# Transposes moved from TensorE to VectorE in a batched x·yᵀ kernel: 32x32 blocks, cross-partition casts and block-diagonal 128x128 weights

## Chip, cores, metric

One core of one Trainium2 chip. The metric is the device time of a whole execution in microseconds (us), median of several runs. The spans in the profiles are about 2 us shorter than these times. In profiles PE is TensorE (matmuls), DVE is VectorE, ACT is ScalarE, POOL is GpSimd, and SP issues the transfers of the 16 DMA engines, which move data in packets. SBUF holds the tiles of these kernels, PSUM the results of their matmuls, and to evict is to copy a result from PSUM to SBUF.

## The reference

```python
x: (8, 12, 512, 64) float32      # batch, heads, t, channels
y: (8, 12, 512, 64) float32      # batch, heads, s, channels
out = np.einsum('bhtc,bhsc->bhts', x, y).astype(np.float32)   # (8, 12, 512, 512)
```

There are 96 independent products of 512x64 by 64x512. The inputs are 25 MB, the output is 101 MB. Both kernels give the matmul its operands with the 64 channels, over which it sums, on partitions, although memory has them along rows. How that transpose is done is what the change is about.

## The kernel before

Twelve groups of eight heads. POOL casts to bf16, TensorE transposes 128x128 blocks into PSUM, VectorE and ScalarE copy them out, TensorE multiplies in 64x64 tiles, VectorE and ScalarE evict, and the SP queue stores 2 MB at a time.

```python
xs = lpool.tile([P, 2, R, C], fp32)                  # R = 16 rows: load runs of 4 KB
nc.sync.dma_start(xs.rearrange("p a r c -> p a (r c)"), xv[g])
...
nc.gpsimd.tensor_copy(b[:, rows], s[:, :, rows].rearrange("p a r c -> p r a c"))   # cast
...
for k in range(K):
    nc.tensor.transpose(pt[:, k, :], yb[:, half * K + k].rearrange("p a c -> p (a c)"), ident)
dst = yT[:, :, half * K:(half + 1) * K]
src = pt.rearrange("p k n -> p n k")                 # scattered read of PSUM, runs of 16 bytes written
nc.vector.tensor_copy(dst, src)                      # or nc.scalar.activation, in turn
...
nc.tensor.matmul(pm[h * 64:(h + 1) * 64, two, :], xT[...], yT[...], start=True, stop=True)
...
if k % 2 == 0: nc.scalar.activation(ot[:, 2 * k:2 * k + 2, :], pm, COPY)
else:          nc.vector.tensor_copy(ot[:, 2 * k:2 * k + 2, :], pm)
nc.sync.dma_start(ov[g, 2 * a + pair], otf)          # 16 KB runs
```

Of the kernel before, what the change touches and what calls it, by code (L numbers as in the profile page):

```python
# [1 line left out]

# [5 lines left out]


@with_exitstack  # L10
def kernel(
    ctx: ExitStack,
    tc: tile.TileContext,
    x: bass.AP,
    y: bass.AP,
    out: bass.AP,
):





    nc = tc.nc
    B, H, T, C = x.shape
    _, _, S, _ = y.shape
    P = 128
    G = 4
    Q = P // G
    R = T // Q
    NG = B * H // (2 * G)  # L30
    K = R // 2
    AHEAD = 3
    fp32 = mybir.dt.float32
    bf16 = mybir.dt.bfloat16
    COPY = mybir.ActivationFunctionType.Copy
    assert C * 2 == P and S == T and R == 16

    xv = x.rearrange("b h t c -> (b h t c)").rearrange("(g a p n) -> g p a n", a=2, p=P, n=R * C)
    yv = y.rearrange("b h t c -> (b h t c)").rearrange("(g a p n) -> g p a n", a=2, p=P, n=R * C)
    ov = out.rearrange("b h t s -> (b h t s)").rearrange("(g a p n) -> g a p n", a=4, p=P, n=K * S)  # L40

    const = ctx.enter_context(tc.tile_pool(name="const", bufs=1))
    lpool = ctx.enter_context(tc.tile_pool(name="lpool", bufs=AHEAD))
    bpool = ctx.enter_context(tc.tile_pool(name="bpool", bufs=2))
    tpool = ctx.enter_context(tc.tile_pool(name="tpool", bufs=2))
    opool = ctx.enter_context(tc.tile_pool(name="opool", bufs=6))
    ptpool = ctx.enter_context(tc.tile_pool(name="ptpsum", bufs=2, space=bass.MemoryType.PSUM))
    pmpool = ctx.enter_context(tc.tile_pool(name="pmpsum", bufs=3, space=bass.MemoryType.PSUM))

    loaded = {}  # L50

    def load(g):
        xs = lpool.tile([P, 2, R, C], fp32)
        ys = lpool.tile([P, 2, R, C], fp32)
        nc.sync.dma_start(ys.rearrange("p a r c -> p a (r c)"), yv[g])  # L55
        nc.sync.dma_start(xs.rearrange("p a r c -> p a (r c)"), xv[g])  # L56
        loaded[g] = (xs, ys)

    for g in range(AHEAD):
        load(g)  # L60

    ident = const.tile([P, P], bf16)
    make_identity(nc, ident)

    def prepare(g, made):

        xs, ys = loaded.pop(g)
        yb = bpool.tile([P, R, 2, C], bf16)
        xb = bpool.tile([P, R, 2, C], bf16)
        for s, b in ((ys, yb), (xs, xb)):  # L70
            for half in range(2):
                rows = slice(half * K, (half + 1) * K)
                nc.gpsimd.tensor_copy(b[:, rows], s[:, :, rows].rearrange("p a r c -> p r a c"))  # L73
        if g + AHEAD < NG:
            load(g + AHEAD)
        yield
        yT = tpool.tile([P, G * Q, R], bf16)
        xT = tpool.tile([P, K, P, 2], bf16)
        for half in range(2):
            pt = ptpool.tile([P, K, P], bf16)  # L80
            for k in range(K):
                nc.tensor.transpose(  # L82
                    pt[:, k, :], yb[:, half * K + k].rearrange("p a c -> p (a c)"), ident
                )
            dst = yT[:, :, half * K:(half + 1) * K]
            src = pt.rearrange("p k n -> p n k")
            if half == 0:
                nc.vector.tensor_copy(dst, src)  # L88
            else:
                nc.scalar.activation(dst, src, COPY)  # L90
            yield
        for half in range(2):
            pt = ptpool.tile([P, K, P], bf16)
            for k in range(K):
                e, i = divmod(k, K // 2)
                nc.tensor.transpose(  # L96
                    pt[:, k, :], xb[:, e * K + half * K // 2 + i].rearrange("p a c -> p (a c)"), ident
                )
            dst = xT[:, half * K // 2:(half + 1) * K // 2]
            src = pt.rearrange("p (e i) n -> p i n e", e=2)  # L100
            if half == 0:
                nc.vector.tensor_copy(dst, src)  # L102
            else:
                nc.scalar.activation(dst, src, COPY)  # L104
            yield
        made[g] = (xT, yT.rearrange("p n k -> p (n k)"))

    made = {}
    for _ in prepare(0, made):
        pass  # L110
    for g in range(NG):
        xT, yT = made.pop(g)
        steps = prepare(g + 1, made) if g + 1 < NG else iter(())
        for a in range(2):
            for pair in range(2):
                ot = opool.tile([P, K, S], fp32)
                otf = ot.rearrange("p r s -> p (r s)")
                edge = (g == 0 and a == 0) or (g == NG - 1 and a == 1)
                for k in range(K // 2):
                    if (pair * K // 2 + k) in (0, 3, 6):  # L120
                        next(steps, None)
                    pm = pmpool.tile([P, 2, S], fp32)
                    for two in range(2):
                        for h in range(2):
                            col = (2 * pair + h) * Q
                            nc.tensor.matmul(  # L126
                                pm[h * 64:(h + 1) * 64, two, :],
                                xT[a * C:(a + 1) * C, 2 * k + two, col:col + Q].rearrange("c n e -> c (n e)"),
                                yT[a * C:(a + 1) * C, (2 * pair + h) * S:(2 * pair + h + 1) * S],
                                start=True, stop=True,  # L130
                            )
                    if k % 2 == 0:
                        nc.scalar.activation(ot[:, 2 * k:2 * k + 2, :], pm, COPY)  # L133
                    else:
                        nc.vector.tensor_copy(ot[:, 2 * k:2 * k + 2, :], pm)  # L135
                    if edge and k % 2 == 1:
                        i, j = (2 * k - 2) * S, (2 * k + 2) * S
                        nc.sync.dma_start(ov[g, 2 * a + pair][:, i:j], otf[:, i:j])
                if not edge:
                    nc.sync.dma_start(ov[g, 2 * a + pair], otf)  # L140


# [1 line left out]
_INS = ['x', 'y']  # L144
_OUTS = [((8, 12, 512, 512), 'float32')]


# [23 lines left out]
```

## Time and profile before

| | before |
|---|---|
| time, median | 306.78 us (3 runs); 306.69 us over the 4 runs beside the changed kernel |
| share of the span in which the DMA engines carry the kernel's data | 98.2% |
| VectorE, ScalarE, POOL busy | 145, 119, 49 us |

The kernel is bound by its DMA; the lines that carry this are in the prediction. Beside them the groups of VectorE: line, engine, operation, tiles, shapes, count, then busy us and mean ns of one.

```profile
L135 DVE COPY ot<-pm 128x1024 f32<-128x1024 f32 x96 | 117.2, 1223 | 113.3 <-PE pm L126 57.3
...
L102 DVE COPY xT<-pt 128x1024 bf16<-128x1024 bf16 x12 | 14.7, 1223 | 10.8 <-PE pt L96 9.4
L88 DVE COPY yT<-pt 128x1024 bf16<-128x1024 bf16 x12 | 14.6, 1216 | 8.9 <-PE pt L82 8.9
```

Three kinds of copy, contiguous and rearranged, cost the same 1.2 us for 1024 elements.

### The profile page before, as it was taken

The page shows a single profiled execution, that of the slowest core. Times are in us where ns is not written, and L with a number is a line of the kernel's source. Part 1 is how long each engine was busy: PE and PEld are TensorE (multiplying, and loading weights), DVE is VectorE, ACT ScalarE, POOL GpSimd, SP SyncE. Part 2 cuts the span into 40 slices and gives each one's busy share as a digit, 9 for nine tenths or more (in the row PEclk, how much of TensorE's full clock was granted, in tenths as well). Part 3 has the DMA queues.
Part 4 walks back from the last instruction along what each step waited for, and adds up shares of the span by engine and source line. Part 5 has one row for each costly group of instructions (what it writes and reads, how often), then busy time and mean ns, then how long its engine had stood idle before and what let it go on. Part 6 is the DMA issues. An engine that isn't in the chain of part 4 may idle for free.

```text
span 304.3 us, 2968 instructions
## 1 busy us (share of the span) xinstructions
PE 208.5 (69%) x1152; PEld 104.6 (34%) x1152; DVE 144.7 (48%) x120; ACT 119.4 (39%) x121; POOL 49.3 (16%) x54
## 2 busy tenths in 40 slices
PE   0899999999959538928946844893897797671000
PEld 0444344555425114513613522541453443330000
DVE  0456666567446435616525733743565664443000
ACT  1454645364445224624515512542364552522000
POOL 3773220400500310230050050031000000000000
PEclk9999999999999855555555655555555555555555
DMA  7999999999999999999999999999999999999992
GB/s 283 411 410 418 436 429 423 419 442 405 445 419 419 430 431 421 420 437 424 426 426 435 414 429 433 413 433 429 433 433 429 431 433 429 428 428 433 423 420 89
DMA packets 14031, 126.03 MB, mean 414 GB/s; under 512 B 1216, under 2 KB 1216, under 8 KB 7360
## 3 DMA queue, kind: packets, MB, share of 16 engines
q1 hardware_dynamic: 14016, 125.83, 98.2%
q8 instruction: 9, 0.15, 0.2%
q14 instruction: 6, 0.05, 0.0%
HBM read 25.17 MB, written 100.66 MB: 413 GB/s over the span
## 4 chain that ended last, share of the span: by engine, by line
DMA 60%; PE 23%; DVE 4%; ACT 2%; issue 1%; POOL 1%; SPq 0%; ACTq 0%
DMA out_dram<-ot 48%; PE pm L126 17%; DMA xs<-in_x_dram 12%; PE pt L82 3%; PE pt L96 3%; DVE ot L135 2%; ACT ot L133 2%; DVE xT L102 1%; POOL xb L73 1%; SPq L55 0%; ACTq L133 0%; SPq L140 0%; ACT xT L104 0%; SPq L56 0%
## 5 line engine op out<-in xcount | busy, mean ns | idle before, releaser
L126 PE MATMUL pm<-yT,xT 64*64 64x512 bf16 x768 | 164.0, 610 | 56.0 <-ACT ot L133 53.9
L135 DVE COPY ot<-pm 128x1024 f32<-128x1024 f32 x96 | 117.2, 1223 | 113.3 <-PE pm L126 57.3
L133 ACT ACTIVATE ot<-pm 128x1024 f32<-128x1024 f32 x96 | 95.1, 1023 | 113.7 <-DMA out_dram<-ot 81.2
L126 PEld LDWEIGHTS <-xT 64*64 64x64 bf16 x768 | 66.1, 150 | 131.2 <-issue 122.7
L73 POOL CAST yb<-ys 128x1024 bf16<-128x1024 f32 x24 | 24.3, 1040 | 140.5 <-DMA ys<-in_y_dram 94.7
L82 PE MATMUL pt<-ident,yb 128*128 128x128 bf16 x192 | 23.7, 307 | 10.7 <-POOL yb L73 6.9
L73 POOL CAST xb<-xs 128x1024 bf16<-128x1024 f32 x24 | 24.3, 1040 | 16.3 <-issue 6.9
L82 PEld LDWEIGHTS <-yb 128*128 128x128 bf16 x192 | 19.9, 143 | 20.3 <-issue 11.5
L96 PE MATMUL pt<-ident,xb 128*128 128x128 bf16 x192 | 24.9, 310 | 1.1 <-POOL xb L73 0.9
L96 PEld LDWEIGHTS <-xb 128*128 128x128 bf16 x192 | 19.1, 141 | 19.3 <-issue 17.8
L104 ACT ACTIVATE xT<-pt 128x1024 bf16<-128x1024 bf16 x12 | 12.3, 1024 | 32.9 <-PE pt L96 29.4
L102 DVE COPY xT<-pt 128x1024 bf16<-128x1024 bf16 x12 | 14.7, 1223 | 10.8 <-PE pt L96 9.4
L88 DVE COPY yT<-pt 128x1024 bf16<-128x1024 bf16 x12 | 14.6, 1216 | 8.9 <-PE pt L82 8.9
L90 ACT ACTIVATE yT<-pt 128x1024 bf16<-128x1024 bf16 x12 | 12.3, 1022 | 9.3 <-PE pt L82 7.7
L90 ACT ACT_TABLE_LOAD x1 | 1.3, 1283 | 0.7 <-PEq L155 0.7
masks.py:199 POOL TENSOR_SCALAR_AFFINE_SELECT ident<-ident 128x128 bf16<-128x128 bf16 x1 | 0.3, 292 | 0.1
masks.py:197 POOL MEMSET ident<- 128x128 bf16 x1 | 0.2, 204 | 0.3 <-POOLq L155 0.3
L155 POOL MEMSET const-float32-0.0<- 128x1 f32 x1 | 0.1, 98 | 0.2 <-issue 0.2
L155 POOL MEMSET const-bfloat16-1.0<- 128x1 bf16 x1 | 0.1, 101 | 0.0
L155 POOL MEMSET const-uint8-127<- 128x1 uint8 x1 | 0.1, 101 | 0.0
L155 POOL MEMSET const-float32-1.0<- 128x1 f32 x1 | 0.1, 98 | 0.0
## 6 DMA issues: line engine op xcount, KB each, us to landing
out_dram<-ot SPq DMA_DIRECT2D x44, 2048.0 KB, 28.3
ys<-in_y_dram SPq DMA_DIRECT2D x12, 1024.0 KB, 20.3
xs<-in_x_dram SPq DMA_DIRECT2D x12, 1024.0 KB, 22.2
out_dram<-ot SPq DMA_DIRECT2D x8, 1024.0 KB, 21.0
```

The lines of the kernel that those rows point to most:

```text
L73: nc.gpsimd.tensor_copy(b[:, rows], s[:, :, rows].rearrange("p a r c -> p r a c"))
L82: nc.tensor.transpose(pt[:, k, :], yb[:, half * K + k].rearrange("p a c -> p (a c)"), ident)
L88: nc.vector.tensor_copy(dst, src)
L90: nc.scalar.activation(dst, src, COPY)
L96: nc.tensor.transpose(pt[:, k, :], xb[:, e * K + half * K // 2 + i].rearrange("p a c -> p (a c)"), ident)
L102: nc.vector.tensor_copy(dst, src)
L104: nc.scalar.activation(dst, src, COPY)
L126: nc.tensor.matmul(pm[h * 64:(h + 1) * 64, two, :], xT[a * C:(a + 1) * C, 2 * k + two, col:col + Q].rearrange("c n e -> c (n e)"), yT[a * ...
L133: nc.scalar.activation(ot[:, 2 * k:2 * k + 2, :], pm, COPY)
L135: nc.vector.tensor_copy(ot[:, 2 * k:2 * k + 2, :], pm)
L155: nc = _bacc.Bacc("TRN2", target_bir_lowering=False, num_devices=1)
```

## The change

The intent is to take the transposes and their evictions off TensorE and PSUM. Two heads share one 128x128 matmul: each is split into two channel halves, the four pieces lie on four blocks of 32 partitions, and the weights hold zeros where the heads differ. VectorE's transpose does this in blocks of 32x32, from SBUF to SBUF. Its output is written so that both operands stand in exactly the order that the matmul wants.

```diff
-    G = 4 ... R = T // Q          # 16 rows per partition and head group
+    G = 8 ... R = T // Q          # 32 rows: load runs of 8 KB
-                nc.gpsimd.tensor_copy(b[:, rows], s[:, :, rows].rearrange("p a r c -> p r a c"))
+        for ch in range(2):
+            for u in range(2):     # 32 partitions at a time, to another block of partitions
+                cast(engines[n % len(engines)], xb[(2 * ch + u) * D:(2 * ch + u + 1) * D, :, :, u, :], ...)
...
-                nc.tensor.transpose(pt[:, k, :], yb[...], ident)      # and the same for x, and evictions
+        nc.vector.transpose(
+            xT.rearrange("p k h m -> p (k h m)").rearrange("p (k r i) -> p k i r", k=K, i=2 * E),
+            xb.rearrange("p k e u c -> p k (e u) c"),
+        )
+        nc.vector.transpose(yT.rearrange("p (r j) -> p j r", j=R), yb)
...
-                                pm[h * 64:(h + 1) * 64, two, :], ...   # 768 matmuls, 64x64
+                    pm[:, two, :], xT[:, k + two, h, :], yT[:, h * S:(h + 1) * S], ...   # 384, 128x128
-                    if k % 2 == 0:  # ScalarE and VectorE in turn
+            if k == 4:              # VectorE one of four, else ScalarE
-    opool bufs=6
+    opool bufs=7
...
+    with tc.manual_schedule():      # instruction order as written; edge stores no longer divided
```

More of the change, by code (lines that the diff above doesn't have):

```diff
@@ L6 @@
 from concourse._compat import with_exitstack
-from concourse.masks import make_identity
 @with_exitstack
@@ L26 @@
     P = 128
-    G = 4
+    G = 8
     Q = P // G
     R = T // Q
-    NG = B * H // (2 * G)
-    K = R // 2
+    NG = B * H // G
+    K = 8
+    E = R // K
+    D = 32
     AHEAD = 3
@@ L35 @@
     COPY = mybir.ActivationFunctionType.Copy
-    assert C * 2 == P and S == T and R == 16
-    xv = x.rearrange("b h t c -> (b h t c)").rearrange("(g a p n) -> g p a n", a=2, p=P, n=R * C)
-    yv = y.rearrange("b h t c -> (b h t c)").rearrange("(g a p n) -> g p a n", a=2, p=P, n=R * C)
-    ov = out.rearrange("b h t s -> (b h t s)").rearrange("(g a p n) -> g a p n", a=4, p=P, n=K * S)
+    assert C == 2 * D and S == T and R == D and Q * 2 == D
+    xv = x.rearrange("b h t c -> (b h t c)").rearrange("(g p n) -> g p n", p=P, n=R * C)
@@ L42 @@
+    yv = y.rearrange("b h t c -> (b h t c)").rearrange("(g p n) -> g p n", p=P, n=R * C)
+    ov = out.rearrange("b h t s -> (b h t s)").rearrange(
+        "(o u h q n) -> o h q u n", u=2, h=2, q=Q * E, n=K * S
+    )
     const = ctx.enter_context(tc.tile_pool(name="const", bufs=1))
     lpool = ctx.enter_context(tc.tile_pool(name="lpool", bufs=AHEAD))
-    bpool = ctx.enter_context(tc.tile_pool(name="bpool", bufs=2))
-    tpool = ctx.enter_context(tc.tile_pool(name="tpool", bufs=2))
-    opool = ctx.enter_context(tc.tile_pool(name="opool", bufs=6))
@@ L47 @@
-    ptpool = ctx.enter_context(tc.tile_pool(name="ptpsum", bufs=2, space=bass.MemoryType.PSUM))
-    pmpool = ctx.enter_context(tc.tile_pool(name="pmpsum", bufs=3, space=bass.MemoryType.PSUM))
-    loaded = {}
+    ybpool = ctx.enter_context(tc.tile_pool(name="ybpool", bufs=2))
+    tpool = ctx.enter_context(tc.tile_pool(name="tpool", bufs=4))
+    opool = ctx.enter_context(tc.tile_pool(name="opool", bufs=7))
+    pmpool = ctx.enter_context(tc.tile_pool(name="pmpsum", bufs=4, space=bass.MemoryType.PSUM))
@@ L52, in load @@
+    loaded, made = {}, {}
+    zeroed = [const.tile([P, K, E, 2, D], bf16, name=f"xb{half}") for half in range(2)]
     def load(g):
-        xs = lpool.tile([P, 2, R, C], fp32)
-        ys = lpool.tile([P, 2, R, C], fp32)
-        nc.sync.dma_start(ys.rearrange("p a r c -> p a (r c)"), yv[g])
-        nc.sync.dma_start(xs.rearrange("p a r c -> p a (r c)"), xv[g])
+        xs = lpool.tile([P, R, C], fp32)
+        ys = lpool.tile([P, R, C], fp32)
+        nc.sync.dma_start(xs.rearrange("p r c -> p (r c)"), xv[g])
+        nc.sync.dma_start(ys.rearrange("p r c -> p (r c)"), yv[g])
@@ L57, in load @@
         loaded[g] = (xs, ys)
-    for g in range(AHEAD):
-        load(g)
-    ident = const.tile([P, P], bf16)
-    make_identity(nc, ident)
-    def prepare(g, made):
-        xs, ys = loaded.pop(g)
-        yb = bpool.tile([P, R, 2, C], bf16)
-        xb = bpool.tile([P, R, 2, C], bf16)
-        for s, b in ((ys, yb), (xs, xb)):
-            for half in range(2):
-                rows = slice(half * K, (half + 1) * K)
-                nc.gpsimd.tensor_copy(b[:, rows], s[:, :, rows].rearrange("p a r c -> p r a c"))
-        if g + AHEAD < NG:
-            load(g + AHEAD)
-        yield
-        yT = tpool.tile([P, G * Q, R], bf16)
-        xT = tpool.tile([P, K, P, 2], bf16)
-        for half in range(2):
-            pt = ptpool.tile([P, K, P], bf16)
-            for k in range(K):
-                nc.tensor.transpose(
-                    pt[:, k, :], yb[:, half * K + k].rearrange("p a c -> p (a c)"), ident
-                )
-            dst = yT[:, :, half * K:(half + 1) * K]
-            src = pt.rearrange("p k n -> p n k")
-            if half == 0:
-                nc.vector.tensor_copy(dst, src)
-            else:
-                nc.scalar.activation(dst, src, COPY)
-            yield
-        for half in range(2):
-            pt = ptpool.tile([P, K, P], bf16)
-            for k in range(K):
-                e, i = divmod(k, K // 2)
-                nc.tensor.transpose(
-                    pt[:, k, :], xb[:, e * K + half * K // 2 + i].rearrange("p a c -> p (a c)"), ident
-                )
-            dst = xT[:, half * K // 2:(half + 1) * K // 2]
-            src = pt.rearrange("p (e i) n -> p i n e", e=2)
-            if half == 0:
-                nc.vector.tensor_copy(dst, src)
-            else:
-                nc.scalar.activation(dst, src, COPY)
-            yield
-        made[g] = (xT, yT.rearrange("p n k -> p (n k)"))
@@ L108 @@
-    made = {}
-    for _ in prepare(0, made):
-        pass
-    for g in range(NG):
-        xT, yT = made.pop(g)
-        steps = prepare(g + 1, made) if g + 1 < NG else iter(())
-        for a in range(2):
-            for pair in range(2):
-                ot = opool.tile([P, K, S], fp32)
-                otf = ot.rearrange("p r s -> p (r s)")
-                edge = (g == 0 and a == 0) or (g == NG - 1 and a == 1)
-                for k in range(K // 2):
-                    if (pair * K // 2 + k) in (0, 3, 6):
-                        next(steps, None)
-                    pm = pmpool.tile([P, 2, S], fp32)
-                    for two in range(2):
-                        for h in range(2):
-                            col = (2 * pair + h) * Q
-                            nc.tensor.matmul(
-                                pm[h * 64:(h + 1) * 64, two, :],
-                                xT[a * C:(a + 1) * C, 2 * k + two, col:col + Q].rearrange("c n e -> c (n e)"),
-                                yT[a * C:(a + 1) * C, (2 * pair + h) * S:(2 * pair + h + 1) * S],
-                                start=True, stop=True,
-                            )
-                    if k % 2 == 0:
-                        nc.scalar.activation(ot[:, 2 * k:2 * k + 2, :], pm, COPY)
-                    else:
-                        nc.vector.tensor_copy(ot[:, 2 * k:2 * k + 2, :], pm)
-                    if edge and k % 2 == 1:
-                        i, j = (2 * k - 2) * S, (2 * k + 2) * S
-                        nc.sync.dma_start(ov[g, 2 * a + pair][:, i:j], otf[:, i:j])
-                if not edge:
-                    nc.sync.dma_start(ov[g, 2 * a + pair], otf)
@@ new lines, in cast, with casts @@
+    def cast(engine, dst, src):
+        if engine is nc.scalar:
+            nc.scalar.activation(dst, src, COPY)
+        else:
+            engine.tensor_copy(dst, src)
+    def casts(g, half, engines):
+        xs, ys = loaded[g]
+        xb = zeroed[half]
+        base = half * 64
+        n = 0
+        for ch in range(2):
+            for u in range(2):
+                lo = base + u * D
+                src = xs[lo:lo + D, :, ch * D:(ch + 1) * D]
+                cast(
+                    engines[n % len(engines)],
+                    xb[(2 * ch + u) * D:(2 * ch + u + 1) * D, :, :, u, :],
+                    src.rearrange("p (e k) c -> p k e c", k=K),
+                )
+                n += 1
+        yb = ybpool.tile([P, R, D], bf16)
+        for ch in range(2):
+            cast(
+                engines[n % len(engines)],
+                yb[ch * 64:(ch + 1) * 64],
+                ys[base:base + 64, :, ch * D:(ch + 1) * D],
+            )
+            n += 1
+        return xb, yb
@@ new lines, in transposes, with result @@
+    def transposes(g, half, xb, yb):
+        xT = tpool.tile([P, K, 2, P], bf16)
+        nc.vector.transpose(
+            xT.rearrange("p k h m -> p (k h m)").rearrange("p (k r i) -> p k i r", k=K, i=2 * E),
+            xb.rearrange("p k e u c -> p k (e u) c"),
+        )
+        yT = tpool.tile([P, 2 * S], bf16)
+        nc.vector.transpose(yT.rearrange("p (r j) -> p j r", j=R), yb)
+        made[g, half] = (xT, yT)
+    def result(g, half, h, steps):
+        xT, yT = made[g, half]
+        ot = opool.tile([P, K, S], fp32)
+        for k in range(0, K, 2):
+            next(steps, None)
+            pm = pmpool.tile([P, 2, S], fp32)
+            for two in range(2):
+                nc.tensor.matmul(
+                    pm[:, two, :], xT[:, k + two, h, :], yT[:, h * S:(h + 1) * S], start=True, stop=True
+                )
+            if k == 4:
+                nc.vector.tensor_copy(ot[:, k:k + 2, :], pm)
+            else:
+                nc.scalar.activation(ot[:, k:k + 2, :], pm, COPY)
+        nc.sync.dma_start(ov[2 * g + half, h], ot.rearrange("p r s -> p (r s)"))
@@ new lines, in prepare @@
+    def prepare(g):
+        b = {}
+        for step in range(16):
+            if step in (0, 1):
+                b[step] = casts(g, step, [nc.gpsimd])
+            if step in (5, 13):
+                transposes(g, step // 8, *b[step // 8])
+            if step == 12 and g + AHEAD < NG:
+                load(g + AHEAD)
+            yield
+    with tc.manual_schedule():
+        for g in range(AHEAD):
+            load(g)
+        nc.vector.memset(zeroed[0], 0.0)
+        nc.gpsimd.memset(zeroed[1], 0.0)
+        b0 = casts(0, 0, [nc.vector, nc.scalar, nc.gpsimd])
+        transposes(0, 0, *b0)
+        b1 = casts(0, 1, [nc.gpsimd, nc.scalar])
+        transposes(0, 1, *b1)
+        if AHEAD < NG:
+            load(AHEAD)
+        for g in range(NG):
+            steps = prepare(g + 1) if g + 1 < NG else iter(())
+            for half in range(2):
+                for h in range(2):
+                    result(g, half, h, steps)
+            for _ in steps:
+                pass
```

## The prediction

> **What bounds the kernel now.** I first read the 40 slices of the span, because the busy shares of the page (PE 69%, DVE 48%, ACT 39%, POOL 16%) name no engine as the limit:
>
> ```profile
> DMA  7999999999999999999999999999999999999992
> GB/s 283 411 410 418 436 429 423 419 442 405 445 419 419 430 431 421 420 437 424 426 426 435 414 429 433 413 433 429 433 433 429 431 433 429 428 428 433 423 420 89
> ...
> q1 hardware_dynamic: 14016, 125.83, 98.2%
> ...
> out_dram<-ot SPq DMA_DIRECT2D x44, 2048.0 KB, 28.3
> ```
>
> From the second slice to the last but one the 16 DMA engines are never idle, and they spend 98.2% of the span on the kernel's own 125.83 MB (25.17 read, 100.66 written). The last line says that a 2 MB store takes 28.3 us from issue to landing. At 430 GB/s 2.10 MB takes 4.88 us, so 28.3/4.88 = 5.8 stores stand in the queue: all six output buffers are full, and the engines run ahead of the DMA as far as buffers allow.
>
> Next the waits, to see whether any engine holds the queue up:
>
> ```profile
> ACT ot L133 <- DMA out_dram<-ot: 81.2, 22, 8.6
> DVE ot L135 <- DMA out_dram<-ot: 55.4, 20, 7.8
> PE pm L126 <- ACT ot L133: 53.9, 21, 8.2
> ```
>
> Both evicting engines wait for a store to free its buffer, 137 us together, and PE waits behind them. Everything queues behind the stores. Then the busy table by stretch, at both ends and in the middle:
>
> ```profile
> 5.00:20.00 15.00, 11.70 (x74) 6.37 (x75) 6.79 (x6) 5.12 (x5) 11.40 (x12) 1.00 1.02 412
> ...
> 200.00:270.00 70.00, 52.21 (x266) 25.82 (x263) 37.76 (x32) 30.05 (x31) 4.05 (x4) 0.50 1.01 430
> 295.00:297.00 2.00, 0.00 (x0) 0.00 (x0) 0.00 (x0) 0.00 (x0) 0.00 (x0) 0.50 0.92 389
> 297.00:300.00 3.00, 0.00 (x0) 0.00 (x0) 0.00 (x0) 0.00 (x0) 0.00 (x0) 0.50 0.34 145
> 300.00:303.00 3.00, 0.00 (x0) 0.00 (x0) 0.00 (x0) 0.00 (x0) 0.00 (x0) 0.50 0.12 49
> ```
>
> Columns: stretch, length, then PE, PEld, DVE, ACT, POOL busy, granted clock, DMA share, GB/s. Three things: the pure-load start runs at 412 GB/s, the store-rich middle at 430; halving the granted PE clock at 100 us changed nothing; and the end is a ramp of 6 us in which only some of the 16 DMA engines still work (49 GB/s is two of them).
>
> The trace's record of single packets says why. Median duration: 4,096 bytes 159 ns, 8,192 bytes 309 ns, 16,384 bytes 611 ns. So each packet costs about 9 ns (2 x 159 - 309) on top of its bytes. The sixteen landings of each DMA say the rest: at the first load the slowest DMA engine is 0.5 us behind the fastest, at the last store 6.6 us[...]. The lag grows in steps, of which the clearest follow packets that are not the kernel's data:
>
> ```profile
> q8 instruction: 9, 0.15, 0.2%
> q14 instruction: 6, 0.05, 0.0%
> ```
>
> Nine packets of 16,384 bytes are 147,456 bytes; PE has 1152 + 1152 instructions, which makes exactly 64 bytes each. So q8 is PE's program being fetched, 256 instructions at a time. Each fetch holds one DMA engine for about 0.94 us, and the lag of that engine jumps by 0.6 to 1.3 us. The slowest engine sets the end.
>
> [...]the trace before has none, but its DVE copies (1024 elements, 1223 ns) give the rate I use[...].
>
> **The change, part by part.** 12 groups of 8 heads as before, per group 2 loads of 1 MB and 4 stores of 2 MB. DMA pace of a group: 2 x 2.45 + 4 x 4.86 = 24.3 us (4.86 is the spacing of 2 MB landings, 2.45 that of the 1 MB stores made of 8 KB packets).
> - Compute per group, against 24.3. POOL: 12 casts of 1024 elements per partition, at 1040 ns each as before (the cost goes by elements per partition, so narrower casts are no cheaper): 12.5 us, up from 4.2. ACT: 12 evictions x 1.023 = 12.3. DVE: 4 evictions x 1.223 = 4.9, plus 2 x (2048-element transpose[...] 2.29, and 1024-element 1.22) = 7.0, sum 11.9. PE: 32 matmuls of 512 columns, at 0.43 each (spacing seen for two of the old ones, an upper value): 13.7. All transposes on PE, their PSUM and their evictions go. Every engine is at half the DMA's pace, so all of this lies beside the DMA: 0 us.
> - Load packets of 8 KB for 4 KB: 6,144 become 3,072. In landings, 1 MB of loads took 2.56 us in the pure-load start and about 2.49 among stores; 8 KB packets took 2.445. Ten loads x 0.11 + fourteen x 0.045 = 1.7 us saved. The edge stores become 16 KB: 8 x 0.015 = 0.1.
> - PE's program: 384 matmuls + 384 weight loads = 768 instructions, 3 fetches for 9. Six fetches of about 1 us fall away from the 16 engines; the slowest engine probably bore three or four of the nine and now one or two. I take 2 us off its lag of 6.6.
> - Start: the first result needs casts, DVE transposes and then ACT, which does casts of the second half first. Loads land at about 5.8 and 8.4 us; casts of the first half end near 9.5, ACT's last cast near 12.5, evictions run until about 16, first store near 16 us. The first eight loads keep the DMA busy until about 22.6 us (23.4 before), so it has 6 us to spare. Next stores by my schedule near 22, 26 and 32 us, due at 27.5, 32 and 37: tight, but fed.
> - End: with seven buffers the last stores are queued some 30 us ahead, so the undivided 2 MB edge stores cost nothing. 0 us.
>
> Sum: -1.8 - 2.0 = -3.8 us; 306.8 - 3.8 = 303.0.
>
> **Rivals.**
> 1. Nothing but the packets counts: lag comes from elsewhere too (part of it grows between fetches, at the loads among stores). For it: all jumps together are 33 us over 16 engines, nine fetches explain perhaps 10. Then about 305.
> 2. The lag shrinks more[...]: the slowest engine lags only 3 us. Then 301, at the edge of 2%.
> 3. POOL becomes the bound. Its casts triple, narrow, and shift between partitions; if a 32-partition cast took twice 1040 ns, POOL would need 25 us per group against 24.3, and the time would be about 315. Against it: the old cast with a permuted source already costs only about 1 ns per element.
> 4. [...]For it: the DRAM side has 64 rows of 2 heads instead of 128.[...] Against it:[...] rows stay 16 KB and the order by partition is kept.
> 5. The start starves the DMA: a delay of the first or second store beyond the 6 us in hand would cost 1 to 4 us.
>
> **Range and chances.** Rivals 1 and 2 set the inside of the range: 301 to 305, widened to 300 and 307 for rival 5 and the run-to-run spread. Faster by over 2% means below 300.8, for which the lag must nearly vanish: 0.17. Slower by over 2% needs rival 3 or 4: 0.12. Within 2%: 0.71.
>
> **What would show it.** Right: DMA slices all at 9 from the second on; 8 KB packets at 309 ns, 16 KB at 611; the instruction queue at 3 packets of 16 KB in place of 9; start stretch above 420 GB/s; ramp at the end of 4 to 5 us instead of 6; POOL near 150 us, ACT near 152, DVE near 143 busy; stores about 6.5 deep. Wrong: a DMA share below 0.9 in the middle (POOL or DVE bound, and SP waiting for evictions while the stores land in 5 to 10 us), 16 KB packets well above 611 ns[...], or a hole between 16 and 40 us (start).

The sum: 1.7 us for load packets and 0.1 for edge stores, 2.0 for PE's program, nothing for compute, together -3.8 us and 303.0. The 2.29 us of the longer transpose belongs to compute; it used a rate that no trace shows; contig_only measured 2.30 later. The trace before has no transpose of VectorE. In rival 2 its 3 us was a guess. Rival 4 is that the new store pattern slows the stores down. That a cast's time goes by its elements per partition was assumed; the page after shows it, 1039 ns on 32 partitions and 1034 on 64, for 1040 on 128 before. The nine fetch packets took 0.89 to 1.11 us each; only after some of them is the slowest DMA engine further behind.

## The result, and the profile after

| | before | after |
|---|---|---|
| time, median | 306.69 us (306.30 to 306.85, 4 runs) | 449.05 us (449.01 to 449.14, 4 runs) |
| ratio | | 1.4645, 95% interval 1.462 to 1.467 |

The outputs are right. All eight runs are fast (none is over 1.5% above the fastest of its kernel). Ratios here and below are the mean time of one kernel's fast runs over that of the other's of the same rounds, so not quite the ratio of the medians. The prediction, 303.0 us and 300 to 307, was far off.

The page of the changed kernel: busy line, two rows of slices, the data queue's share, store landings.

```profile
PE 140.9 (32%) x384; PEld 49.7 (11%) x384; DVE 384.8 (86%) x99; ACT 144.6 (32%) x150; POOL 144.1 (32%) x142
...
DVE  5999999999889898898898988988989889889630
...
DMA  8904399597688498298298487667844826628497
...
q1 hardware_dynamic: 10368, 125.83, 68.1%
...
out_dram<-ot SPq DMA_DIRECT2D x48, 2048.0 KB, 7.8
```

The DMA row, a wall of nines before, is full of holes; 68.1% replaces 98.2%. A store lands 7.8 us after its issue in place of 28.3, so the queue is nearly empty. VectorE is busy nearly everywhere. ScalarE and POOL, at 145 and 144 us, are near what I had worked out (152 and 150); VectorE is at 385 in place of 143. Its groups say where:

```profile
L98 DVE STREAM_TRANSPOSE xT<-xb 128x2048 bf16<-128x2048 bf16 x24 | 222.3, 9263 | 0.3 <-ACT xb L66 0.3
...
L103 DVE STREAM_TRANSPOSE yT<-yb 128x1024 bf16<-128x1024 bf16 x24 | 115.9, 4828 | 0.0
L118 DVE COPY ot<-pm 128x1024 f32<-128x1024 f32 x48 | 62.8, 1313 | 41.1 <-issue 36.2
```

The transposes take 9.26 and 4.83 us; I had 2.29 and 1.22. Together that is 338 us, more than the whole kernel before. The waits follow from it:

```profile
ACT ot L120 <- PE pm L114: 281.0, 52, 11.6
PE pm L114 <- DVE ot L118: 265.9, 25, 12.6
POOL xb L68 <- DVE xT L98: 225.7, 22, 11.3
```

ScalarE waits for matmuls, matmuls wait for VectorE's one eviction in four, and POOL waits for the transpose to free its buffer: each wait is up to 12 us long, about as long as a pair of transposes. VectorE's order in time (start us, us) shows one half group (four heads, two stores):

```profile
206.00 1.23 DVE L118 COPY ot<-pm 128x1024 f32<-128x1024 f32 x1 [2.01 <-issue]
207.14 9.26 DVE L98 STREAM_TRANSPOSE xT<-xb 128x2048 bf16<-128x2048 bf16 x1
216.03 4.83 DVE L103 STREAM_TRANSPOSE yT<-yb 128x1024 bf16<-128x1024 bf16 x1
220.52 1.40 DVE L118 COPY ot<-pm 128x1024 f32<-128x1024 f32 x1
223.93 1.22 DVE L118 COPY ot<-pm 128x1024 f32<-128x1024 f32 x1 [2.01 <-issue]
```

From 206.00 to 223.93 are 17.93 us per half group. 24 x 17.93 = 430 us, and about 17 us of start and end make the span of 447. Of the period, 13.4 us are the transposes from start to start, 2.5 the evictions, and 2.0 are idle: the eviction is queued behind the transposes, the matmuls stand until it frees PSUM, and VectorE then waits for the matmuls that it held up.

One rival of mine, the store pattern, is dead at this point. Where the changed kernel stores back to back, its 2 MB stores land 4.8 to 4.9 us apart by the trace, as before, and a 16 KB packet takes 615 ns (median) against 611. The new store pattern, 64 x 2 rows, shows no cost.

### The profile page after: what moved, and what is told of

Read it like the earlier page. It is cut to its first block, busy times and chain, and to the rows that moved or that the text cites. A ratio compares the mean times of both kernels' runs of the same rounds, so it can differ in the third digit from the quotient of the medians.

```text
span 447.1 us, 1551 instructions
## 1 busy us (share of the span) xinstructions
PE 140.9 (32%) x384; PEld 49.7 (11%) x384; DVE 384.8 (86%) x99; ACT 144.6 (32%) x150; POOL 144.1 (32%) x142
## 3 DMA queue, kind: packets, MB, share of 16 engines
q1 hardware_dynamic: 10368, 125.83, 68.1%
## 5 line engine op out<-in xcount | busy, mean ns | idle before, releaser
L114 PE MATMUL pm<-yT,xT 128*128 128x512 bf16 x384 | 140.9, 541 | 288.8 <-DVE ot L118 265.9
L120 ACT ACTIVATE ot<-pm 128x1024 f32<-128x1024 f32 x144 | 138.0, 1029 | 281.4 <-PE pm L114 281.0
L98 DVE STREAM_TRANSPOSE xT<-xb 128x2048 bf16<-128x2048 bf16 x24 | 222.3, 9263 | 0.3 <-ACT xb L66 0.3
L68 POOL CAST xb<-xs 32x1024 bf16<-32x1024 f32 x91 | 94.5, 1039 | 232.2 <-DVE xT L98 225.7
L103 DVE STREAM_TRANSPOSE yT<-yb 128x1024 bf16<-128x1024 bf16 x24 | 115.9, 4828 | 0.0
L118 DVE COPY ot<-pm 128x1024 f32<-128x1024 f32 x48 | 62.8, 1313 | 41.1 <-issue 36.2
L114 PEld LDWEIGHTS <-xT 128*128 128x128 bf16 x384 | 49.7, 130 | 379.4 <-issue 351.3
L68 POOL CAST yb<-ys 64x1024 bf16<-64x1024 f32 x46 | 47.5, 1034 | 7.7 <-DVE yT L103 2.7
L68 DVE CAST xb<-xs 32x1024 bf16<-32x1024 f32 x2 | 2.1, 1058 | 3.8 <-DMA xs<-in_x_dram 3.7
L66 ACT ACTIVATE xb<-xs 32x1024 bf16<-32x1024 f32 x3 | 3.2, 1053 | 0.1
## 6 DMA issues: line engine op xcount, KB each, us to landing
ys<-in_y_dram SPq DMA_DIRECT2D x12, 1024.0 KB, 11.9
```

The costliest lines, as they stand in the source:

```text
L66: nc.scalar.activation(dst, src, COPY)
L68: engine.tensor_copy(dst, src)
L98: nc.vector.transpose(xT.rearrange("p k h m -> p (k h m)").rearrange("p (k r i) -> p k i r", k=K, i=2 * E), xb.rearrange("p k e u c -> p k ...
L103: nc.vector.transpose(yT.rearrange("p (r j) -> p j r", j=R), yb)
L114: nc.tensor.matmul(pm[:, two, :], xT[:, k + two, h, :], yT[:, h * S:(h + 1) * S], start=True, stop=True)
L118: nc.vector.tensor_copy(ot[:, k:k + 2, :], pm)
```

## The experiments

The question is why the transposes take four times what I gave them. **Theory A**: they write SBUF in scattered 2-byte elements. **Theory B**: the transpose of 2-byte elements is slow by itself. **Theory C**: it is held up by POOL or the DMA beside it. For A speaks the diff beside the trace before: the copies there write contiguously or in runs of 16 bytes, at 1.22 us for 1024 elements, while the change writes single 2-byte elements 16 and 64 bytes apart. I had not looked at that before predicting.

### 1. The disputed cost by itself

```diff
+ # in short; the run has one loop for each kind
+ for s in (1, 2, 4, 8, 16, 32):       # step between consecutive written elements, bf16
+     nc.vector.transpose(t_out.rearrange("p (b i j) -> p b j i", i=32, j=s), src in order)
+ # the same as plain copies, in fp32, with scattered reads, and beside 40 POOL casts
```

> A bare series of VectorE transposes of 128x1024 bf16, one kind after another, no stores and no matmuls beside them; results are not the reference's. Theory A (the scattered write is what costs: the changed kernel's transposes put consecutive elements 16 and 64 bytes apart): written contiguously (t_out1) about 1.2 us, t_out8 and t_out32 about 4.8 us as in the changed kernel[...]. Theory B (the transpose of 2-byte elements is slow by itself): 4.8 us in every kind, contiguous too. Theory C[...]: everything about 1.2 us while POOL is idle, and p_out1 and p_out8, beside POOL's casts, about 4.8 us. Plain copies with the same steps (c_out8, c_out32): slow too if it is the write, fast if it is the transpose. t_in8 (scattered read, contiguous write): about 1.2 us under A if only writes suffer[...].

The groups of this kernel; the sources' lines tell the kinds apart: L43, 46, 49, 52, 55, 58 write in steps of 2, 4, 8, 16, 32, 64 bytes; L61 reads in steps of 16; L64 and L67 are copies in steps of 2 and 16; L76 is a transpose of fp32 in steps of 32; L84 and L87 are L43 and L52 again beside POOL.

```profile
L87 DVE STREAM_TRANSPOSE p_out<-src 128x1024 bf16<-128x1024 bf16 x4 | 18.9, 4724 | 0.1
L52 DVE STREAM_TRANSPOSE t_out<-src 128x1024 bf16<-128x1024 bf16 x3 | 14.1, 4706 | 0.1
L58 DVE STREAM_TRANSPOSE t_out<-src 128x1024 bf16<-128x1024 bf16 x3 | 14.0, 4674 | 0.1
L55 DVE STREAM_TRANSPOSE t_out<-src 128x1024 bf16<-128x1024 bf16 x3 | 13.5, 4513 | 0.1
...
L67 DVE COPY c_out<-src 128x1024 bf16<-128x1024 bf16 x3 | 7.3, 2429 | 0.1
L49 DVE STREAM_TRANSPOSE t_out<-src 128x1024 bf16<-128x1024 bf16 x3 | 7.3, 2425 | 0.1
L76 DVE STREAM_TRANSPOSE f_out<-xs 128x1024 f32<-128x1024 f32 x3 | 6.0, 2000 | 0.1
L61 DVE STREAM_TRANSPOSE t_in<-src 128x1024 bf16<-128x1024 bf16 x3 | 5.9, 1979 | 0.1
L84 DVE STREAM_TRANSPOSE p_out<-src 128x1024 bf16<-128x1024 bf16 x4 | 5.0, 1244 | 0.1
...
L46 DVE STREAM_TRANSPOSE t_out<-src 128x1024 bf16<-128x1024 bf16 x3 | 3.9, 1291 | 0.1
L43 DVE STREAM_TRANSPOSE t_out<-src 128x1024 bf16<-128x1024 bf16 x3 | 3.7, 1246 | 0.1
L64 DVE COPY c_out<-src 128x1024 bf16<-128x1024 bf16 x3 | 1.2, 413 | 0.1
```

Contiguous, the transpose takes 1.25 us, as I had assumed. At 16 bytes and above it takes 4.5 to 4.7, about as in the changed kernel (4.83). B is refuted, and so is C as far as this bench goes: POOL beside it changes nothing (1244 and 4724 ns), and the slow transposes are slow although no DMA ran. The time goes up with the step of the write and then stays: 1.25 us contiguous, 1.29 at 4 bytes, 2.43 at 8, 4.7 at 16, 4.5 and 4.7 at 32 and 64. The rate is not the same for every write, though: in steps of 32 bytes the fp32 transpose took 2.00 us (1.31 contiguous), and in steps of 16 the VectorE copy 2.43. Experiment 7 comes back to this.

### 2. The write alone, in place

```diff
         nc.vector.transpose(
-            xT.rearrange("p k h m -> p (k h m)").rearrange("p (k r i) -> p k i r", k=K, i=2 * E),
-            xb.rearrange("p k e u c -> p k (e u) c"),
+            xT.rearrange("p k h m -> p (k h m)"),
+            xb.rearrange("p k e u c -> p (k e u c)"),
         )
-        nc.vector.transpose(yT.rearrange("p (r j) -> p j r", j=R), yb)
+        nc.vector.transpose(yT, yb.rearrange("p r c -> p (r c)"))
```

> The changed kernel with one edit: both transposes write contiguously; the numbers come out in the wrong order, so the result is wrong on purpose. Theory A: transposes 2.3 us and 1.2 us for 9.26 and 4.83, VectorE from 385 to about 145 us busy, DMA never idle after the start, time about 303 us (300 to 306), which is what my prediction's sum gives when its one wrong figure is put right. Theory B: 9.26 and 4.83 us stay, time stays at 449.

Its output is wrong, which doesn't matter for the time. Measured: 305.21 us (304.72 to 305.35), ratio to the kernel before 0.9953 (0.9937 to 0.997). The page and its groups:

```profile
DMA  7999999999999999999999999999999999999991
...
L98 DVE STREAM_TRANSPOSE xT<-xb 128x2048 bf16<-128x2048 bf16 x24 | 55.3, 2303 | 4.6 <-POOL xb L68 4.3
...
L103 DVE STREAM_TRANSPOSE yT<-yb 128x1024 bf16<-128x1024 bf16 x24 | 28.9, 1203 | 0.0
```

2303 and 1203 ns are the 2.29 and 1.22 us of my prediction, and with them the DMA row is nines again. The DMA is busier here than in the changed kernel (97.8% of the span for 68.1%), so the DMA part of C is out too. The output patterns of two transposes are the whole loss of 144 us. A second time, beside experiment 5's last kernel:

> contig_only once more, with more rounds and beside steps8b, wrong on purpose as before: to size what the change's plan is worth without scattered writes. 305.2 us, ratio to the kernel before 0.995 to 0.997. steps8b should lie within 0.5 us of it if the remaining difference is noise of starts.

Measured: 304.47 us (304.24 to 305.59), ratio 0.9936 (0.9921 to 0.995).

### 3. POOL out of the way

```diff
-                b[step] = casts(g, step, [nc.gpsimd])
+                b[step] = casts(g, step, [nc.scalar])
```

> The changed kernel with the steady casts on ScalarE in place of POOL, so POOL is idle beside the transposes. Theory C (contention with POOL): transposes fall towards 2.3 and 1.2 us and the time drops far below 449. Theories A and B: transposes stay at 9.26 and 4.83 us within 3%, time within a few per cent of 449, a little more since evictions queue behind casts on ScalarE (about 290 us busy).

Measured: 447.06 us in one run, result correct. The transposes did not move, so POOL is refuted in place too:

```profile
L98 DVE STREAM_TRANSPOSE xT<-xb 128x2048 bf16<-128x2048 bf16 x24 | 222.5, 9272 | 0.3 <-ACT xb L66 0.3
...
L103 DVE STREAM_TRANSPOSE yT<-yb 128x1024 bf16<-128x1024 bf16 x24 | 115.7, 4821 | 0.0
```

### 4. Does VectorE alone set the pace?

```diff
-            if k == 4:
-                nc.vector.tensor_copy(ot[:, k:k + 2, :], pm)
-            else:
-                nc.scalar.activation(ot[:, k:k + 2, :], pm, COPY)
+            nc.scalar.activation(ot[:, k:k + 2, :], pm, COPY)
```

> The changed kernel with all evictions on ScalarE: VectorE does nothing but transposes. If VectorE alone sets the pace: 24 x (9.26 + 4.83) = 338 us plus about 20 us of start and end, so 355 to 362 us. If instead a ring of waits sets it (casts waiting for the transpose to free their buffer, matmuls waiting for evictions), the half-group period stays near 17.9 us and the time above 420. ScalarE goes to about 190 us busy and does not bind.

Measured: 353.69 us in one run, correct; just below the 355 to 362 expected. VectorE is busy 94% of the span with transposes alone:

```profile
PE 143.1 (41%) x384; PEld 49.4 (14%) x384; DVE 329.3 (94%) x51; ACT 185.1 (53%) x198; POOL 144.4 (41%) x142
```

So of the 142 us, 95 went with 48 evictions of about 1.3 us and the idle times that they caused by standing in VectorE's queue: 63 us of copies and 41 us of idle time in the page after, less 9 us by which the transposes themselves took longer here. The long waits in the page after are effects, not a second cause.

### 5. Correct kernels without the scattered write

A contiguous transpose leaves the elements in another order, which someone else must put right. For y there are two ways: the matmul takes columns as they come and the eviction puts them right, or the matmul reads them scattered. (x, whose transposed form is the weights, stays as it is in these two.)

```diff
-        nc.vector.transpose(yT.rearrange("p (r j) -> p j r", j=R), yb)
+        nc.vector.transpose(yT, yb.rearrange("p r c -> p (r c)"))
 # y_fix_evict:
-   rhs yT[:, h * S:(h + 1) * S];  eviction pm -> ot
+   rhs yT.rearrange("p (r i) -> p r i", i=D)[:, :, h * Q:(h + 1) * Q]
+   eviction pm.rearrange("p t (r q) -> p t q r", q=Q) -> ot, all on ScalarE
 # y_fix_pe:
+   rhs yT.rearrange("p (r i) -> p i r", i=D)[:, h * Q:(h + 1) * Q, :];  eviction plain, all on ScalarE
```

> A correct kernel: only the y transpose writes contiguously, its columns then come out of the matmul in another order, and the evictions, now all on ScalarE, put them back by reading PSUM 64 bytes apart. VectorE has 9.26 + 1.2 = 10.5 us per half group, below the DMA's 12.15, so the theory says DMA-bound again, 305 to 307 us, if a scattered PSUM read costs ScalarE nothing (as the transposed evictions of the kernel before: 1022 and 1024 ns against 1023). If it costs twice or more, ScalarE needs over 16 us per half group and the time goes to 400 or above.

Measured: 308.36 us (306.92 to 308.75), ratio 1.0053 (1.0033 to 1.0073), correct; above the 305 to 307 expected. ScalarE's eviction takes 1043 ns with the scattered PSUM read against 1030 without (contig_only), so that is nearly free. The kernel is again bound by the DMA, but for its start: 236 GB/s between 20 and 25 us, worth about 5 x (1 - 236/428) = 2.2 us, and 398 GB/s between 30 and 60 us, worth another 2.1 us. The x transposes there still take 9.3 us each, which is the likely reason; no run shows it.

> The same, but the matmul reads y in the right order from steps of 64 bytes and the evictions stay plain, all on ScalarE. If PE reads a scattered moving operand at full rate (matmul spacing 0.43 us or less) the time is 305 to 307 us; if scattered reads cost PE what scattered writes cost VectorE, a matmul takes 1.5 us or more, PE becomes the bound at 16 x 1.5 = 24 us per half group and the time is near 600 us.

Measured: 358.0 us (357.96 to 358.05), ratio 1.1682 (1.1665 to 1.1699), correct. The PE group:

```profile
L114 PE MATMUL pm<-yT,xT 128*128 128x512 bf16 x384 | 329.1, 1033 | 18.4 <-DVE yT L103 18.4
```

PE is never idle once it has begun: 329.1/384 = 0.86 us per matmul at full granted clock. That misses both of my figures (0.43 or 1.5). Single columns read 64 bytes apart cost TensorE twice the time here (the matmuls of the changed kernel follow each other every 0.43 us), and it becomes the bound. In y_fix_evict, which reads runs of 16 columns (32 bytes), PE is busy 0.40 us per matmul (41.14 us for 102 between 200 and 270 us).

For x, the step can be halved: with 16 rows per partition in place of 32, 32 partitions of one head give the 32 outputs of a block, and the step is i = 4 elements, 8 bytes.

```diff
# in short: the start, the buffer counts and the order of heads change with it
-    G = 8 ... Q = P // G            # 16 partitions per head, 32 rows, 8 KB load runs
+    G = 8 ... Q = 32                # 32 partitions per head, 16 rows, 4 KB load runs
-            xT... "p (k r i) -> p k i r", i=2 * E      # E = 4: steps of 16 bytes
+            xT... "p (k r i) -> p k i r", i=2 * E      # E = 2: steps of 8 bytes
-        nc.vector.transpose(yT.rearrange("p (r j) -> p j r", j=R), yb)
+        nc.vector.transpose(yT, yb.rearrange("p r c -> p (r c)"))
-                nc.scalar.activation(ot[:, k:k + 2, :], pm, COPY)
+                nc.scalar.activation(dst, pm.rearrange("p t (r q) -> p t q r", q=Q), COPY)
```

> A correct kernel that keeps the change's idea (block-diagonal weights, VectorE transposes, no transposes on PE) but lays a partition out as 16 rows in place of 32, so that the transposed x is written in steps of 8 bytes in place of 16; y is written contiguously and put right by the evictions; load runs are 4 KB again. From the sweep of steps: an x transpose of 1024 elements 2.43 us, a y transpose of 512 about 0.7, so per store 3.1 + one eviction 1.2 = 4.3 us of VectorE against 6.1 us of DMA. If the write step alone decides, the DMA never idles after the start and the time is 305 to 306 us, at or just below the kernel before (306.5). If the steps cost more beside the other work than alone (over 5 us for the x transpose), VectorE binds again and the time is above 330.

Measured: 307.33 us (307.04 to 307.65), ratio 1.0031 (1.0017 to 1.0046), and wrong, by a fault of mine in the order of its first group, told in the next text. The x transpose took 2452 ns.

> steps8 with its start mended. In steps8 casts of the second group overwrote buffers of the first that were still to be transposed (a fault of mine: 2 of 48 stores wrong, which is the relative error 0.288 = sqrt(2 x 2/48)), and VectorE waited there for casts, which left the DMA at 317 GB/s between 30 and 40 us. Now correct, and without that hole, which cost about 2.6 us: 305 us (304.3 to 305.7), just faster than the kernel before (306.5). The x transpose stays at 2.45 us and the y transpose at 0.71. If the hole stays, 307.

Measured: 304.51 us (304.11 to 305.27), ratio 0.9928 (0.9915 to 0.9941), correct. That is 0.7% below the kernel before, clear of the noise of these runs though far from 2%, and 32% below the changed kernel.

```profile
DMA  7999999999999999999999999999999999999992
...
L96 DVE STREAM_TRANSPOSE xT<-xb 128x1024 bf16<-128x1024 bf16 x48 | 117.6, 2449 | 2.2 <-POOL xb L68 1.4
...
L101 DVE STREAM_TRANSPOSE yT<-yb 128x512 bf16<-128x512 bf16 x48 | 34.1, 710 | 0.0
```

2449 ns is about the 2425 of the sweep at 8 bytes. VectorE is at 193 us of 303 and hidden behind the DMA.

### 6. The two small terms of my sum

With the big error out of the way, contig_only can size the gains that I had promised. Load packets:

```diff
-        nc.sync.dma_start(xs.rearrange("p r c -> p (r c)"), xv[g])
+        for part in range(2):       # and the same for y: two column halves, 4 KB runs
+            cols = slice(part * R * C // 2, (part + 1) * R * C // 2)
+            nc.sync.dma_start(xs.rearrange("p r c -> p (r c)")[:, cols], xv[g][:, cols])
```

> contig_only with every load cut into two column halves, so the load packets are 4 KB again as in the kernel before (6,144 for 3,072), wrong on purpose as contig_only is. This sizes the term of my sum for load packets, worked out as 1.7 us. In contig_only a pure-load megabyte lands every 2.48 us against 2.56 in the kernel before, so 24 x 0.08 = 1.9 us at most. If the term is right, about 306.5 to 307 us against 305.2 for contig_only; if packet size of loads does not matter for the end, 305.2 within 0.4.

Measured: 305.17 us (304.46 to 306.02), ratio 0.996 (0.9946 to 0.9974). With 8 KB packets it was 0.9953 and 0.9936: no difference that stands out. The test is not pure: each load is now two transfers, and contig_4k moves 188 GB/s over its first 5 us where contig_only moves 213, while its slowest DMA engine ends 4.0 us behind the fastest and not 6.0. steps8b agrees, though: it loads 4 KB runs and took 304.51 us beside contig_only's 304.47 in the same rounds.

PE's program:

```diff
             for two in range(2):
+                for _ in range(2):
+                    nc.tensor.matmul(pm[0:1, two, 0:1], xT[:, k + two, h, 0:1], yT[:, h * S:h * S + 1], start=True, stop=True)
                 nc.tensor.matmul(pm[:, two, :], ...)
```

> contig_only with two one-column matmuls ahead of each real one, so PE runs 2304 instructions as in the kernel before (9 program fetches of 16 KB in place of 3), wrong on purpose. This sizes the term for PE's program, taken as 2 us. If fetches set the lag of the slowest DMA engine, the instruction queue shows 9 packets, the ramp at the end grows from contig_only's and the time is 306 to 307.5 us; if they don't, 305.2 within 0.4. PE must not bind (about 23 us per group at most by the matmul spacing of 0.43 us, against 24.3).

Measured: 306.09 us (305.95 to 307.42), ratio 0.9995 (0.9981 to 1.0009). The stretches at the end (columns as in the prediction), first contig_only, then contig_pad with its instruction queue:

```profile
297.00:300.00 3.00, 0.00 (x0) 0.00 (x0) 0.00 (x0) 0.00 (x0) 0.00 (x0) 0.50 0.20 87
300.00:303.00 3.00, 0.00 (x0) 0.00 (x0) 0.00 (x0) 0.00 (x0) 0.00 (x0) 0.50 0.06 27
```

```profile
q8 instruction: 9, 0.15, 0.2%
```

```profile
297.00:300.00 3.00, 0.00 (x0) 0.00 (x0) 0.00 (x0) 0.00 (x0) 0.00 (x0) 1.00 0.33 142
300.00:303.50 3.50, 0.00 (x0) 0.00 (x0) 0.00 (x0) 0.00 (x0) 0.00 (x0) 1.00 0.09 37
```

The queue shows nine fetches again, the ramp is longer, and by the landings of the last store the slowest DMA engine is 6.9 us behind the fastest, against 6.0 and 4.9 in the two runs of contig_only and 6.6 in the kernel before. Against contig_only's three ratios (0.9953, 0.9936, and 0.996 with 4 KB loads) that is 1.1 to 1.8 us for six fetches, with 0.4 to 0.5 us of uncertainty on each ratio. It is not a pure test: the padding also kept PE busy for 243 us (137 in contig_only) and its granted clock at 1.0, and the evictions now wait more for PE (168 us) than for stores (62). For the fetches speaks that the DMA row stays at nines, with a store landing 30.8 us after its issue.

### 7. Whose law is it?

```diff
+ # in short; the run has one loop for each kind
+ nc.vector.tensor_copy / nc.scalar.activation / nc.gpsimd.tensor_copy of bf16, written in steps of 2, 4, 8, 16, 64 bytes
+ nc.vector.transpose reading in steps of 4, 8, 16, 64 bytes, writing contiguously
```

> Same bench as stride_sweep, wrong on purpose, other kinds: VectorE transposes that read in steps of 4, 8, 16 and 64 bytes and write contiguously; VectorE, ScalarE and POOL copies of bf16 that write in steps. [...]copies by the other engines slow down at the same steps (ScalarE and POOL from about 1.0 us to 2 us or more at 16 bytes). If only VectorE's write side is slow there, ScalarE and POOL stay at 1.0 to 1.1 us for all steps. Reads: 1.25 us at 4 and 8 bytes, 2.0 at 16 and 64, as the one read measured (1.98 at 16 bytes).

In the names, the number is the step in elements of 2 bytes: vc VectorE copies, ac ScalarE, pc POOL, rd transposes with scattered reads.

```profile
L58 DVE COPY vc4x<-src 128x1024 bf16<-128x1024 bf16 x3 | 17.0, 5656 | 0.1
...
L88 POOL COPY pc8x<-src 128x1024 bf16<-128x1024 bf16 x3 | 15.0, 5007 | 0.1
L73 ACT ACTIVATE ac8x<-src 128x1024 bf16<-128x1024 bf16 x3 | 14.3, 4779 | 0.1
...
L55 DVE COPY vc2x<-src 128x1024 bf16<-128x1024 bf16 x3 | 11.1, 3696 | 0.1
L70 ACT ACTIVATE ac4x<-src 128x1024 bf16<-128x1024 bf16 x3 | 7.5, 2492 | 0.1
L85 POOL COPY pc4x<-src 128x1024 bf16<-128x1024 bf16 x3 | 7.4, 2478 | 0.1
L61 DVE COPY vc8x<-src 128x1024 bf16<-128x1024 bf16 x3 | 7.3, 2441 | 0.1
L49 DVE STREAM_TRANSPOSE rd8x<-src 128x1024 bf16<-128x1024 bf16 x3 | 6.0, 2009 | 0.1
...
L67 ACT ACTIVATE ac2x<-src 128x1024 bf16<-128x1024 bf16 x3 | 4.0, 1340 | 0.1
L82 POOL COPY pc2x<-src 128x1024 bf16<-128x1024 bf16 x3 | 4.0, 1335 | 0.1
...
L46 DVE STREAM_TRANSPOSE rd4x<-src 128x1024 bf16<-128x1024 bf16 x3 | 3.7, 1232 | 0.1
L64 ACT ACTIVATE ac1x<-src 128x1024 bf16<-128x1024 bf16 x3 | 3.2, 1057 | 4.4 <-DVE src L35 4.4
L79 POOL COPY pc1x<-src 128x1024 bf16<-128x1024 bf16 x3 | 3.1, 1039 | 6.1 <-DVE src L35 6.0
```

ScalarE and POOL slow down at the same steps as the transpose: 2.5 us at 8 bytes and 4.8 to 5.0 at 16, so by these times handing the scattered write to a copy on one of them would not have helped. Already at 4 bytes they take 1.34 us for 1.05. Scattered reads cost the transpose less: nothing at 8 bytes (1.23 us), 2.0 us at 16.

So the slow write is not the transpose's alone. What causes it is not shown, and VectorE's plain copies go another way: 0.41 us contiguous, 3.70 at 4 bytes, 5.66 at 8 and 2.44 at 16. At 4 and 8 bytes they are slower than every other kind, and at 16 they take half of what ScalarE and POOL take (4.78 and 5.01). So does the fp32 transpose of experiment 1 (2.00 us at 32 bytes, for 4.51 in bf16). Why stays open; no run was made for it.

## Why the prediction was wrong

- **What bounds the kernel before**: right. Each variant whose engines keep up ends between 304.5 and 308.4 us, with the DMA row at nines but for the holes at the start named above.
- **The step that failed** is the cost of the two transposes, "2.29, and 1024-element 1.22". I took it from copies that write SBUF contiguously or in runs of 16 bytes, and did not look at the output pattern in the diff, which writes single 2-byte elements 16 and 64 bytes apart. (The way from 1.22 to 2.29 used a rate that no trace here shows; for contiguous writes contig_only confirms both, 1203 and 2303 ns.) Measured: 9.26 and 4.83 us. VectorE's sum for a group, 7.0 + 4.9 = 11.9 us, becomes 2 x 14.1 + 4 x 1.3 = 33.4 us against the DMA's 24.3. With that, "every engine is at half the DMA's pace" fell, and VectorE became the bound. Experiment 2 puts the term right and nothing else, and gives 305.21 and 304.47 us.
- **What came on top**: the evictions that VectorE does in order behind its transposes stop the matmuls and cost 2 us of idle time per half group. I had not thought of that, as it only exists once VectorE is late. Experiment 4 measures the evictions with their idle time as 95 us.
- **The other engines** were right: POOL 144 us for "near 150", ScalarE 145 for "near 152", the narrow casts at 1039 ns for 1040.
- **The rivals**: I gave POOL (3) and the store pattern (4) the 12% for a slow outcome, and no rival was a slow VectorE operation, although the text itself says that the trace before has no DVE transpose. That is where the doubt belonged. Both rivals were refuted by the profile after. Only the list of signs names "POOL or DVE bound", and its sign came as written: DMA share below 0.9 (68.1% over the span), SP waiting 357 us for VectorE's evictions, stores landing in 7.8 us. (A slip beside it: 2% below 306.8 is 300.7, not 300.8.)
- **Load packets, 1.7 us**: nothing in the end (contig_4k, and steps8b with 4 KB loads). Single landings do come faster at the start, 2.48 us per MB for 2.56, yet the eighth load of contig_only landed 22.2 us after the first packet against 21.9 in the kernel before. The gain goes as the stores begin: between 20 and 24 us contig_only moves 315 and 352 GB/s at a DMA share of 0.89 and 0.88, where the kernel before moves 410. That is a small case of rival 5, a start that does not quite feed the DMA; no run varied it.
- **PE's program, 2 us**: the fetches fell from nine to three as forecast, and contig_pad puts six of them at 1.1 to 1.8 us, in a test that is not pure. But I had taken the lag from 6.6 to 4.6 us, and with three fetches it is still 4.0 to 6.2 us (contig_4k, contig_only twice, steps8b). Most of the lag comes from elsewhere, as rival 1 had it.
- **Start**: the first store was issued at 16.3 us in contig_only, as worked out ("near 16 us").

So the change without its write pattern is worth 1.4 to 2 us, 0.5 to 0.6%, where I had said 3.8.

## What to carry to other kernels

When a layout is changed, follow the innermost step of every write into SBUF, in bytes. For bf16 here, against a contiguous write, steps of 4 bytes cost a transpose 4% more (1.29 us for 1.25) and a copy on ScalarE or POOL 27 to 28% more (1.34 for 1.06 and 1.04), steps of 8 bytes 1.9 to 2.4 times the time, steps of 16 to 64 bytes 3.6 to 5.4 times. VectorE's plain copies keep no such order (nine times at 4 bytes, fourteen at 8, six at 16, against 0.41 us for their contiguous form), so measure them. Put the reordering where it is cheap: here that was the read of PSUM by the eviction (1043 ns for 1030), not the transpose's write (9.26 us for 2.30) and not the matmul's moving operand (0.86 us for 0.43). And when an added instruction has no duration in the trace before, put the doubt of the prediction there.
